# FFN entry of a decoder step: two pairs evicted unscaled, a table loaded earlier, weight sums queued behind an eviction

## The chip, the cores and the metric

The kernel runs on one core of a Trainium2 chip. The metric is the device time of one execution in microseconds. Before the change it is 1154.72 us, the median of three runs (1151.85 to 1155.08).

## The reference, cut to what matters

One layer of a hybrid decoder is computed in float32 for 520 tokens (a prompt of 512 and 8 single samples) of width 1024. A retention branch and a gated spatial branch (whose gate inputs go through Gelu) are merged and added to the residual. The change lies where the feed-forward part begins:

```python
hn = rms_norm(h, norm_ffn_g)                       # h * rsqrt(mean(h*h) + eps) * g, per token
f_gate, f_up = jnp.split(hn @ w_ffn_in, 2, axis=-1) # 1024 -> 2 x 2816
h = h + (silu(f_gate) * f_up) @ w_ffn_down          # 2816 -> 1024
```

Afterwards comes one last RMSNorm.

## The kernel before

**Layout.** Activations lie with features on the 128 partitions and the 520 tokens along the free dimension, in two halves L and R of 260. Every float32 product is three matmuls on split operands (high times high, high times low, low times high). A split is a cast on ScalarE (L87, `whi`, `hxh`) and a subtraction on VectorE (L90, `wlo`, `hxl`).

**Phases near the change.** In order: eight products `ps_gu` with Gelu (L691), `ps_gm`, the merged projection `ps_wo` (its eviction into `hs` is L844), then the feed-forward part. That part has 22 pairs (one block of 128 gate columns and one of 128 up columns each), run as pairs 0 to 9, a down projection `ps_fd`, pairs 10 to 17, a second down phase, pairs 18 to 21, and a third. In a down phase each of eight blocks is evicted by L906 (times the root) and added to `hs` by L907.

**One pair.** `ffn_in(i)` uses a seven-product scheme (Strassen's, on the 2 x 2 blocks of gate and up against the two halves of the model width, with the tokens' halves). `seven` runs seven stages of 12 matmuls each (L822), in the order a, s1, b, s2, s3, s4, d, into three accumulators:

```python
into = dict(a=0, b=2, s1=1, s2=0, s3=0, s4=1, d=0)
```

Banks 0 and 1 are one two-bank tile `ps_f`, of which two exist, bank 2 is a tile of its own, `ps_f3`. Behind each stage `seen` evicts: s1 by L874 (ScalarE), s2 by L876 (ScalarE), b by L872 (VectorE, times the root `rstd`), s3 by L878 (VectorE), s4 by L880 (VectorE), then L881 (GpSimd, times `rstd`, half R) and Silu (L882, ScalarE), d by L884 (ScalarE), and L885 (GpSimd) multiplies gate and up. A stage that writes `ps_f` waits for the eviction of the stage before it, even when that one read the tile's other bank. So s4 waits for L878, and d for L880; stages of the next pair fill such gaps where they are ready.

**Sums of weights.** The scheme needs sums of weight blocks. `sum_weights` loads `ab` and `d` on SP's queue (L747, L749), and `s13` by two SP loads and an adding DMA from GpSimd's queue (L744, L745), and makes `s24` by two additions on VectorE:

```python
nc.vector.tensor_tensor(out=s24[:, 0], in0=s13[:, 0], in1=ab[:, 0], op=ALU.add)      # L753
nc.vector.tensor_tensor(out=s24[:, 1], in0=s24[:, 0], in1=ab[:, 1], op=ALU.add)      # L754
```

`s24`, `s13` and `ab` are split into high and low parts for the stages. There are four buffers of each kind and a pair takes three, in turn. So the cast of a pair's `s24` waits for the buffer of the `s13` of the pair before, which that pair's s3 is the last to read.

**The root.** `row_rstd` (L148 to L155) makes `rstd` from the rows' sums of squares: a scaling on VectorE, Abs_reciprocal_sqrt on ScalarE (L152), and three VectorE instructions that refine it (L153, L154, L155). It is traced behind stage a of pair 0. `rsqrt_table` runs that function on one column so that its table is loaded early. Before, the call that precedes the feed-forward part reads the last Sigmoid's output `sg`; the Gelus, which use another table, run after it.

**Order of work.** Each engine runs its instructions in a fixed order, which a planner writes: it goes through a simulated time, and takes on each engine the earliest traced instruction that is ready. Nothing but data and buffers binds L753, so in the order before, the sums of a pair can stand ahead of evictions of the pair before it. In the order planned, the stages of the entry follow each other as a(0), a(1), s1(0), b(0), b(1) with s2(0), s1(1), s3(0), s4(0), s2(1), d(0), s3(1), a(2). Later pairs alternate between s3(2), s1(3), b(3), s4(2), s2(3), d(2) and s3(3), a(4), s4(3), s1(4), b(4), d(3), s2(4).

Of the kernel before, what the change touches and what calls it, by code (L numbers as in the profile page):

```python
# [7 lines left out]
F32 = mybir.dt.float32  # L8
# [3 lines left out]
ALU = mybir.AluOpType  # L12
# [3 lines left out]
KT = D // P  # L16
NP = 512
NS = 8
T = NP + NS
HT = T // 2  # L20
# [15 lines left out]
def halves(ap):  # L36
    return ap.rearrange("p (a b) -> p a b", a=2)
# [3 lines left out]
def step_kernel(ctx: ExitStack, tc: tile.TileContext, io):  # L41
    nc = tc.nc
# [13 lines left out]
    def ttile(name):  # L56
        return tmp.tile([P, T], F32, name=name, tag="tmp")

    def pair(name):
        return big.tile([P, 2, T], F32R, name=name, tag="big")  # L60
# [7 lines left out]
    def acc_psum(name):  # L68
        return psm.tile([P, 2, 512], F32, name=name, tag="mm")

    def aux(name):
        return psa.tile([P, 512], F32, name=name, tag="aux")
# [4 lines left out]
    def wtile(kind, dt=F32R):  # L77

        pools = wpools[kind]
        pool = pools[wturn[kind] % len(pools)]  # L80
        wturn[kind] += 1
        return pool.tile([P, 8 * P], dt, name=kind, tag=kind, bufs=pools.count(pool))

    def split(hi, lo, src, hi_eng=None, lo_eng=None):

        if hi_eng is None:
            nc.scalar.copy(out=hi, in_=src)  # L87
        else:
            hi_eng.tensor_copy(out=hi, in_=src)
        (lo_eng or nc.vector).tensor_tensor(out=lo, in0=src, in1=hi.bitcast(F32), op=ALU.subtract)  # L90
# [39 lines left out]
    def rsqrt_table(after):  # L130

        one = small.tile([P, 1], F32, name="one", bufs=1)
        nc.scalar.activation(out=one, in_=after[:, 0:1], func=AF.Abs_reciprocal_sqrt)
# [10 lines left out]
    def row_rstd(out, ps, width):  # L144

        y, v, t = (stile(f"rr_{x}") for x in "yvt")
        for f in range(2):
            nc.vector.tensor_scalar(  # L148
                out=v[:, f * HT : (f + 1) * HT], in0=ps[f][:, 0:HT], scalar1=1.0 / width, scalar2=EPS,
                op0=ALU.mult, op1=ALU.add,  # L150
            )
        root = nc.scalar.activation(out=y, in_=v, func=AF.Abs_reciprocal_sqrt)  # L152
        nc.vector.scalar_tensor_tensor(out=t, in0=y, scalar=-0.5, in1=y, op0=ALU.mult, op1=ALU.mult)  # L153
        nc.vector.tensor_tensor(out=t, in0=t, in1=v, op=ALU.mult)  # L154
        nc.vector.scalar_tensor_tensor(out=out, in0=t, scalar=1.5, in1=y, op0=ALU.add, op1=ALU.mult)  # L155
        return root
# [8 lines left out]
    def row_sums(acc):  # L165

        pr = [stile(f"sq{x}", F32R) for x in "hl"]
        split(pr[0], pr[1], acc)
        out = []
        for f in range(2):  # L170
            ps = aux("ps_ss")
            for k in range(2):
                nc.tensor.matmul(
                    ps[:, 0:HT], ones_r, pr[k][:, f * HT : (f + 1) * HT], start=k == 0, stop=k == 1
                )
            out.append(ps)
        return out
# [21 lines left out]
    rstd = const.tile([P, T], F32, name="rstd")  # L199
# [498 lines left out]
    sg = []  # L698
    with tc.tile_pool(name="gp", bufs=1) as gp:
        gm = gmlp(gp)  # L700


    rsqrt_table(sg[-1][:, 1, :])
    mm = []
    for i in range(KT):
        w = weights(io["w_gm_o"][i], KT)
# [3 lines left out]
        s = ttile("ms")  # L710
# [17 lines left out]

    fp = ctx.enter_context(tc.tile_pool(name="fp", bufs=1))

    def sum_weights(src):

        def block(t):
            return t.rearrange("p (a b) -> p a b", a=2)

        def both(t):
            hi, lo = wtile("whi"), wtile("wlo")
            split(hi, lo, t)
            hi, lo = block(hi), block(lo)
            return [(hi[:, i], lo[:, i]) for i in range(2)]  # L740

        s13 = block(wp.tile([P, 8 * P], F32, name="s13", tag="wraw", bufs=3))
        for i in range(2):
            nc.sync.dma_start(out=s13[:, i], in_=src[:, 0])  # L744
        nc.gpsimd.dma_start(out=s13, in_=src[:, 1:3], accum_op=ALU.add)  # L745
        ab = block(wq.tile([P, 8 * P], F32, name="ab", tag="wraw", bufs=2))
        nc.sync.dma_start(out=ab, in_=src[:, 2:4])  # L747
        d = fp.tile([P, 4 * P], F32, name="d", bufs=1)
        nc.sync.dma_start(out=d, in_=src[:, 1])  # L749
        w = dict(zip("a b".split(), both(ab.rearrange("p a b -> p (a b)"))))  # L750
        w |= dict(zip("s1 s3".split(), both(s13.rearrange("p a b -> p (a b)"))))
        s24 = block(fp.tile([P, 8 * P], F32, name="s24", bufs=1))
        nc.vector.tensor_tensor(out=s24[:, 0], in0=s13[:, 0], in1=ab[:, 0], op=ALU.add)  # L753
        nc.vector.tensor_tensor(out=s24[:, 1], in0=s24[:, 0], in1=ab[:, 1], op=ALU.add)  # L754
        w |= dict(zip("s2 s4".split(), both(s24.rearrange("p a b -> p (a b)"))))
        w["d"] = tuple(wq.tile([P, 4 * P], F32R, name=f"wd{x}") for x in "hl")
        split(*w["d"], d)
        return w
# [51 lines left out]
    def seven(w, x, name, seen):  # L810

        ps = acc_psum(name)
        bank = [ps[:, 0, 0:HT], ps[:, 1, 0:HT], aux(f"{name}3")[:, 0:HT]]
        into = dict(a=0, b=2, s1=1, s2=0, s3=0, s4=1, d=0)
        begun = {2}
        for s in ORDER:
            to = into[s]
            acts = x[MEETS[s]]
            for k, (xh, xl) in enumerate(acts):
                sl = slice(k * P, (k + 1) * P)  # L820
                for n, (ww, xx) in enumerate(((w[s][0], xh), (w[s][0], xl), (w[s][1], xh))):
                    nc.tensor.matmul(  # L822
                        bank[to], ww[:, sl], xx, start=to not in begun,
                        stop=k == len(acts) - 1 and n == 2, skip_group_check=True,
                    )
                    begun.add(to)
            if s == "a":
                nc.scalar.copy(out=bank[2], in_=bank[0])
            seen(s, bank)
# [6 lines left out]
    for i in range(KT):  # L836
# [6 lines left out]
        hi = hs[:, i, :]  # L843
# [11 lines left out]
    hx = sum_acts(fill_h, "hx", KT // 2)  # L855
# [2 lines left out]

    rstd = const.tile([P, T], F32, name="rstd")
    act = []  # L860
    L, R = slice(0, HT), slice(HT, T)

    def ffn_in(i):

        a, b = ttile("fa"), ttile("fb")

        def seen(s, bank):
            if s == "a":
                if i == 0:
                    row_rstd(rstd, row_sums(sq), D)  # L870
            elif s == "b":
                nc.vector.tensor_tensor(out=a[:, L], in0=bank[2], in1=rstd[:, L], op=ALU.mult)  # L872
            elif s == "s1":
                nc.scalar.activation(out=b[:, R], in_=bank[1], func=AF.Copy, scale=-1.0)  # L874
            elif s == "s2":
                nc.scalar.copy(out=a[:, R], in_=bank[0])  # L876
            elif s == "s3":
                nc.vector.tensor_tensor(out=b[:, R], in0=b[:, R], in1=bank[0], op=ALU.subtract)  # L878
            elif s == "s4":
                nc.vector.tensor_tensor(out=a[:, R], in0=a[:, R], in1=bank[1], op=ALU.add)  # L880
                nc.gpsimd.tensor_tensor(out=a[:, R], in0=a[:, R], in1=rstd[:, R], op=ALU.mult)  # L881
                nc.scalar.activation(out=a, in_=a, func=AF.Silu)  # L882
            else:
                nc.scalar.activation(out=b[:, L], in_=bank[0], func=AF.Copy, scale=-1.0)  # L884
                nc.gpsimd.tensor_tensor(out=b, in0=a, in1=b, op=ALU.mult)  # L885

        seven(sum_weights(io["w_ffn_in"][i].rearrange("p (s c) -> p s c", s=4)), hx, "ps_f", seen)
        pr = pair(f"act{i}")
        split(pr[:, 0, :], pr[:, 1, :], b)
        act.append(pr)  # L890

    def down(ps, w, k0, n, fs=(0, 1)):
        for k in range(n):
            product(ps, w, k, act[k0 + k], k == 0, k == n - 1, fs)

    def down_weights(i, k0, n):
        return weights(io["w_ffn_down"][i][:, k0 * P : (k0 + n) * P], n)

    def ffn_down(k0, n, last=False):

        for i in range(KT - last):
            ps = acc_psum("ps_fd")
            down(ps, down_weights(i, k0, n), k0, n)
            hi = hs[:, i, :]
            t = ttile("fd")
            nc.vector.tensor_tensor(out=halves(t), in0=ev(ps), in1=halves(rstd), op=ALU.mult)  # L906
            nc.vector.tensor_tensor(out=hi, in0=hi, in1=t, op=ALU.add)  # L907
            if last:

                add_square(sq, hi, i == 0, add=nc.vector)  # L910
                nc.scalar.activation(out=hi, in_=hi, func=AF.Copy, scale=gains[:, 2, i : i + 1])

    done = k0 = 0
    for n in (8, 8, 6):
        for i in range(done, min(k0 + NACT, NF)):
            ffn_in(i)
        done = min(k0 + NACT, NF)
# [8 lines left out]
    i = KT - 1  # L926
    hi = hs[:, i, :]
# [112 lines left out]
```

## Time and profile before

| | |
|---|---|
| median of three runs | 1154.72 us |
| the profiled execution | 1151.46 us |
| its span, first to last instruction | 1149.8 us |
| TensorE busy | 1116.9 us (97%) |
| VectorE busy | 760.9 us (66%) |
| ScalarE busy | 513.5 us (45%) |
| GpSimd busy | 225.1 us (20%) |
| mean granted TensorE clock | 0.989 |

PE is TensorE's matmuls and PEld its weight loads, DVE is VectorE, ACT ScalarE, POOL GpSimd, SP the queue of SyncE. Times count from the first instruction. The feed-forward part begins at about 766 us, its down phases lie at about 873 to 922, 1002 to 1053 and 1097 to 1133 us.

### The profile page before, as it was taken

To read this page: it belongs to the slowest core of one execution; us is meant where nothing else is said; L and a number is where in the kernel's file an instruction comes from. 1 tells how busy PE (TensorE), PEld (TensorE's weight loads), DVE (VectorE), ACT (ScalarE), POOL (GpSimd) and SP (SyncE) were. 2 spreads that over 40 slices of the span, in tenths; PEclk is the share of its full clock that TensorE was granted. 3 is DMA by queue.
4 is the path that set the end of the run, shared out by engine and by line. 5 is a ranking of instruction groups with operands and counts; after the bars stand their busy time and mean duration, and the time that the engine had idled before them with its cause. 6 is when DMAs were issued, how large, how long until landed. Compare 5 with 4: busy or idle time off the path is not lost.

```text
span 1149.8 us, 21702 instructions
## 1 busy us (share of the span) xinstructions
PE 1116.9 (97%) x8982; PEld 1095.4 (95%) x8982; DVE 760.9 (66%) x1223; ACT 513.5 (45%) x837; POOL 225.1 (20%) x198
## 2 busy tenths in 40 slices
PE   8999999999999999999999999998999999999994
PEld 7999999999999999999999999998999999999993
DVE  7777837885788578648534456697786467645754
ACT  6365345533554356323322432465664155522551
POOL 4303201320142011001211222222332013310200
PEclk8999999999999999999999999999999999999998
DMA  7267336733673367222222322665655556445302
GB/s 269 99 233 265 112 111 217 251 111 111 241 245 105 112 231 275 80 94 82 89 79 83 109 80 93 171 137 142 176 150 149 138 126 187 138 122 140 90 18 74
DMA packets 54434, 164.82 MB, mean 143 GB/s; under 512 B 6416, under 2 KB 8864, under 8 KB 54328
## 3 DMA queue, kind: packets, MB, share of 16 engines
q1 hardware_dynamic: 43488, 124.53, 32.7%
q0 software_dynamic: 10848, 38.91, 12.4%
q8 instruction: 70, 1.15, 0.4%
q14 instruction: 28, 0.23, 0.1%
HBM read 142.32 MB, written 21.10 MB: 142 GB/s over the span
## 4 chain that ended last, share of the span: by engine, by line
PE 71%; DVE 12%; DMA 7%; issue 5%; ACT 3%; POOL 1%; SPq 0%; DVEq 0%; ACTq 0%; POOLq 0%
PE ps_f L822 15%; PE ps_fd L108 10%; PE ps_ro L108 8%; PE ps_v L108 7%; PE ps_gu L108 4%; PE ps_ar L108 4%; PE ps_gm L108 4%; PE ps_ag L108 3%; PE ps_gv L108 3%; DVE wlo L90 3%; DMA S<-in_st 3%; PE q L108 2%; PE k L108 2%; PE ps_g L108 2%; PE ps_sc L363 1%
## 5 line engine op out<-in xcount | busy, mean ns | idle before, releaser
L87 ACT CAST whi<-wraw 128x1024 fp32r<-128x1024 f32 (+3 forms) x139 | 141.3, 1018 | 275.2 <-issue 60.1
L90 DVE TENSOR_TENSOR wlo<-wraw,whi 128x1024 fp32r<-128x1024 f32 (+3 forms) x139 | 182.7, 1315 | 33.3 <-ACT whi L87 31.2
L108 PE MATMUL ps_fd<-act,whi 128*128 128x260 f32 x704 | 113.7, 282 | 2.4 <-DVE fd L906 1.8
L822 PE MATMUL ps_f<-hxh,whi 128*128 128x260 f32 x352 | 101.1, 287 | 6.1 <-DVE fb L878 3.9
L108 PEld LDWEIGHTS ps_fd<-act,whi 128*128 128x128 f32 x704 | 96.6, 188 | 3.4 <-ACT whi L87 1.6
L822 PE MATMUL ps_f<-hxh,wlo 128*128 128x260 f32 x352 | 99.3, 284 | 0.6 <-DVE wlo L90 0.6
L822 PE MATMUL ps_f<-hxl,whi 128*128 128x260 f32 x352 | 99.8, 284 | 0.0
L108 PE MATMUL ps_ro<-gated,whi 128*128 128x260 f32 x512 | 82.5, 283 | 0.0
L108 PE MATMUL ps_g<-xg,whi 128*128 128x260 f32 x512 | 82.5, 283 | 0.0
L108 PE MATMUL ps_v<-xg,whi 128*128 128x260 f32 x512 | 82.0, 282 | 0.0
L822 PEld LDWEIGHTS ps_f<-hxh,whi 128*128 128x128 f32 x352 | 66.7, 190 | 8.8 <-DVE fb L878 4.5
L108 PE MATMUL ps_fd<-act,wlo 128*128 128x260 f32 x352 | 71.8, 282 | 0.0
L108 PEld LDWEIGHTS ps_ro<-gated,whi 128*128 128x128 f32 x512 | 70.5, 188 | 0.8 <-issue 0.2
L108 PEld LDWEIGHTS ps_v<-xg,whi 128*128 128x128 f32 x512 | 70.0, 188 | 0.0
L108 PEld LDWEIGHTS ps_g<-xg,whi 128*128 128x128 f32 x512 | 69.8, 188 | 0.0
L822 PEld LDWEIGHTS ps_f<-hxh,wlo 128*128 128x128 f32 x352 | 66.5, 190 | 0.8 <-DVE wlo L90 0.8
L447 ACT ACTIVATE kv<-qkb,vs 128x256 f32<-128x256 f32 x128 | 54.0, 498 | 29.0 <-DMA qkb<-qks 26.0
L822 PEld LDWEIGHTS ps_f<-hxl,whi 128*128 128x128 f32 x352 | 66.7, 190 | 0.0
L90 DVE TENSOR_TENSOR wlo<-s,whi 128x1024 fp32r<-128x1024 f32 x44 | 58.3, 1324 | 12.0 <-ACT whi L87 12.0
L822 PE MATMUL ps_f<-hxm,whi 128*128 128x260 f32 x352 | 65.8, 283 | 0.0
L87 ACT CAST whi<-s 128x1024 fp32r<-128x1024 f32 x44 | 46.1, 1048 | 40.3 <-PE ps_fd L108 20.5
L452 DVE SCALAR_TENSOR_TENSOR junk<-S,qkb 128x256 f32<-128x256 f32 x128 | 53.8, 421 | 2.2
(271 smaller groups left out, 2884.4 us busy)
## 6 DMA issues: line engine op xcount, KB each, us to landing
wraw<-in_w_in SPq DMA_DIRECT2D x78, 512.0 KB, 3.5
S<-in_st SPq DMA_DIRECT2D x32, 512.0 KB, 4.9
out_rss<-S POOLq DMA_DIRECT2D x32, 512.0 KB, 3.9
s<-in_w_ffn_in SPq DMA_DIRECT2D x44, 256.0 KB, 4.2
s<-in_w_ffn_in POOLq DMA_DIRECT2D x22, 512.0 KB, 6.3
ab<-in_w_ffn_in SPq DMA_DIRECT2D x22, 512.0 KB, 4.4
qkb<-qks POOLq DMA_DIRECT2D x16, 512.0 KB, 5.0
wraw<-in_w_ret_o SPq DMA_DIRECT2D x16, 512.0 KB, 3.5
```

The source lines that it names most:

```text
L87: nc.scalar.copy(out=hi, in_=src)
L90: (lo_eng or nc.vector).tensor_tensor(out=lo, in0=src, in1=hi.bitcast(F32), op=ALU.subtract)
L108: nc.tensor.matmul((ps[f] if isinstance(ps, list) else ps[:, f])[:, 0:HT], a, x[:, k, f * HT : (f + 1) * HT], start=first and n == 0, stop ...
L363: nc.tensor.matmul(ps[:, 0:n], a[:, d, s * P : (s + 1) * P], b[:, d, s * P : NP], start=i == 0, stop=i == 5)
L447: nc.scalar.activation(out=kv[:, j, :], in_=kb, func=AF.Copy, scale=vs[:, j, b : b + 1])
L452: nc.vector.scalar_tensor_tensor(out=junk, in0=S[:, j, :], scalar=1.0, in1=qb, op0=ALU.mult, op1=ALU.mult, accum_out=os_[:, j, b : b + 1],)
L822: nc.tensor.matmul(bank[to], ww[:, sl], xx, start=to not in begun, stop=k == len(acts) - 1 and n == 2, skip_group_check=True,)
```

## The change

- The early table load now reads the low half of the last Gelu's product, so it comes behind the last Gelu.
- For pairs 0 and 1, L872 copies bank 2 without `rstd`; L881 then multiplies all 520 columns of `fa` by `rstd`, and not the R half alone.
- L878's instructions are kept in a list, with the L907 of the second last block of each down phase (the last one before the special end in the third). The first addition of a pair's `s24` (L753) is ordered, on VectorE's queue alone, behind the last entry of that list when the pair is traced. For pairs 1 to 9, 11 to 17 and 19 to 21 that is the L878 of the pair before; for pairs 10 and 18 it is that L907. Pair 0 has none.

```diff
-    rsqrt_table(sg[-1][:, 1, :])
+    rsqrt_table(gm[-1][:, 1, :].bitcast(F32))
...
-    def sum_weights(src):
+    def sum_weights(src, behind):
...
-        nc.vector.tensor_tensor(out=s24[:, 0], in0=s13[:, 0], in1=ab[:, 0], op=ALU.add)
+
+        with tc.issue_after(behind.ins) if behind else nullcontext():
+            nc.vector.tensor_tensor(out=s24[:, 0], in0=s13[:, 0], in1=ab[:, 0], op=ALU.add)
...
+    evicted = []
...
             elif s == "b":
-                nc.vector.tensor_tensor(out=a[:, L], in0=bank[2], in1=rstd[:, L], op=ALU.mult)
+                if i < 2:
+                    nc.vector.tensor_copy(out=a[:, L], in_=bank[2])
+                else:
+                    nc.vector.tensor_tensor(out=a[:, L], in0=bank[2], in1=rstd[:, L], op=ALU.mult)
...
             elif s == "s3":
-                nc.vector.tensor_tensor(out=b[:, R], in0=b[:, R], in1=bank[0], op=ALU.subtract)
+                evicted.append(nc.vector.tensor_tensor(out=b[:, R], in0=b[:, R], in1=bank[0], op=ALU.subtract))
             elif s == "s4":
                 nc.vector.tensor_tensor(out=a[:, R], in0=a[:, R], in1=bank[1], op=ALU.add)
-                nc.gpsimd.tensor_tensor(out=a[:, R], in0=a[:, R], in1=rstd[:, R], op=ALU.mult)
+                cols = slice(0 if i < 2 else HT, T)
+                nc.gpsimd.tensor_tensor(out=a[:, cols], in0=a[:, cols], in1=rstd[:, cols], op=ALU.mult)
                 nc.scalar.activation(out=a, in_=a, func=AF.Silu)
...
-        seven(sum_weights(io["w_ffn_in"][i].rearrange("p (s c) -> p s c", s=4)), hx, "ps_f", seen)
+        seven(sum_weights(io["w_ffn_in"][i].rearrange("p (s c) -> p s c", s=4), evicted and evicted[-1]), hx, "ps_f", seen)
...
-            nc.vector.tensor_tensor(out=hi, in0=hi, in1=t, op=ALU.add)
+            done = nc.vector.tensor_tensor(out=hi, in0=hi, in1=t, op=ALU.add)
+            if i == KT - 2:
+                evicted.append(done)
```

## Rows read from the trace of the kernel before

**Rows 1.** The page, busy time, share of the span and instructions by engine.

```profile
PE 1116.9 (97%) x8982; PEld 1095.4 (95%) x8982; DVE 760.9 (66%) x1223; ACT 513.5 (45%) x837; POOL 225.1 (20%) x198
```

**Rows 2.** Busy time by stretch: length, PE, PEld, DVE, ACT, POOL; clock, DMA share, GB/s.

```profile
766.00:776.00 10.00, 8.30 (x68) 7.91 (x67) 8.55 (x17) 6.88 (x15) 0.99 (x1) 1.00 0.50 105
776.00:780.80 4.80, 4.80 (x42) 4.70 (x40) 2.20 (x4) 2.94 (x4) 0.00 (x0) 1.00 0.38 109
780.80:783.70 2.90, 0.12 (x1) 0.00 (x0) 2.87 (x6) 1.53 (x3) 0.85 (x1) 1.00 0.25 23
783.70:787.20 3.50, 3.44 (x16) 3.44 (x17) 2.85 (x7) 0.64 (x1) 0.00 (x0) 0.52 0.70 136
792.00:873.00 81.00, 80.82 (x670) 80.19 (x670) 61.26 (x77) 48.79 (x79) 27.09 (x21) 1.00 0.60 160
```

**Rows 3.** Timeline of TensorE: start, duration, instruction, [idle before, releaser].

```profile
769.32 0.36 PE L822 MATMUL ps_f<-hxh,whi 128*128 128x260 f32 x1 [1.14 <-DVE hs L844]
...
770.36 0.39 PE L822 MATMUL ps_f<-hxh,wlo 128*128 128x260 f32 x1 [0.56 <-DVE wlo L90]
...
783.76 0.59 PE L822 MATMUL ps_f<-hxh,whi 128*128 128x260 f32 x1 [2.85 <-DVE fb L878]
...
934.84 0.39 PE L822 MATMUL ps_f<-hxh,whi 128*128 128x260 f32 x1 [0.52 <-DVE fb L878]
...
1035.77 0.72 PE L108 MATMUL ps_fd<-act,whi 128*128 128x260 f32 x4 [1.46 <-DVE fd L906]
```

**Rows 4.** Timeline of VectorE ahead of the entry.

```profile
764.46 0.69 DVE L753 TENSOR_TENSOR s<-s,ab 128x512 f32<-128x512 f32 x1
...
767.55 0.68 DVE L754 TENSOR_TENSOR s<-s,ab 128x512 f32<-128x512 f32 x1
...
768.49 0.68 DVE L844 TENSOR_TENSOR hs<-ps_wo,xr 128x520 f32<-128x520 f32 x1
```

**Rows 5.** Timeline of ScalarE: the kernel's start, behind the last Gelu, the entry.

```profile
4.24 0.64 ACT L161 ACTIVATE sq<-xt 128x520 f32<-128x520 f32 x1 [0.76 <-DMA xt<-in_xT]
...
680.84 1.05 ACT L87 CAST whi<-wraw 128x1024 fp32r<-128x1024 f32 x1 [3.26 <-PE ps_gm L108]
...
777.83 0.38 ACT L876 COPY fa<-ps_f 128x260 f32<-128x260 f32 x1 [2.17 <-PE ps_f L822]
778.23 1.28 ACT L152 ACT_TABLE_LOAD   x1
```

**Rows 6.** Timeline of VectorE at the entry, from the root on.

```profile
780.20 0.70 DVE L153 SCALAR_TENSOR_TENSOR rr_t<-rr_y 128x520 f32<-128x520 f32 x1 [2.60 <-ACT rr_y L152]
...
781.55 1.22 DVE L90 TENSOR_TENSOR wlo<-ab,whi 128x1024 fp32r<-128x1024 f32 x1
782.68 0.69 DVE L155 SCALAR_TENSOR_TENSOR rstd<-rr_t,rr_y 128x520 f32<-128x520 f32 x1
783.29 0.42 DVE L878 TENSOR_TENSOR fb<-fb,ps_f 128x260 f32<-128x260 f32 x1
...
784.76 0.75 DVE L872 TENSOR_TENSOR fa<-ps_f,rstd 128x260 f32<-128x260 f32 x2
```

**Rows 7.** GpSimd's products (min/median/max ns), its addition at the entry, VectorE beside it.

```profile
L881 POOL TENSOR_TENSOR fa<-fa,rstd x22: 744/1128/1666, 787.3 to 1096.9; 128x260 f32<-128x260 f32 x22
L885 POOL TENSOR_TENSOR fb<-fa,fb x22: 1302/1472/1786, 791.7 to 1099.1; 128x520 f32<-128x520 f32 x22
765.38 1.61 POOL L163 TENSOR_TENSOR sq<-sq,sqr 128x520 f32<-128x520 f32 x1
765.07 2.22 DVE L788 TENSOR_TENSOR xsum<-xsum 128x260 f32<-128x260 f32 x1
```

**Rows 8.** Timelines of ScalarE and VectorE behind s3 of pair 2: split of pair 3's s24.

```profile
803.28 1.05 ACT L87 CAST whi<-s 128x1024 fp32r<-128x1024 f32 x1 [0.70 <-PE ps_f L822]
804.37 1.23 DVE L90 TENSOR_TENSOR wlo<-s,whi 128x1024 fp32r<-128x1024 f32 x1 [0.54 <-ACT whi L87]
```

**Rows 9.** Timeline of VectorE in the second down phase.

```profile
1033.59 0.69 DVE L753 TENSOR_TENSOR s<-s,ab 128x512 f32<-128x512 f32 x1 [8.18 <-DMA s<-in_w_ffn_in]
```

## The prediction

> **What bounds the kernel now.** The page comes first: TensorE is busy 1116.9 of 1149.8 us [rows 1], so only the roughly 33 us in which it isn't, and stretches in which it runs slowly, can be won without taking matmuls away. VectorE's 66% is no second bound over the whole span. The reader then goes to the busy times by stretch: between 792 and 873 us, with pairs 2 to 9 in flight, TensorE is busy 80.82 of 81 us with 670 matmuls, 0.1206 us each [rows 2]. A stage of 12 matmuls is therefore 1.45 us, and a steady pair has nothing to give. The entry is different: 8.30 busy of 10 us (766 to 776), 0.12 of 2.90 (780.8 to 783.7), and then 16 matmuls in 3.44 us at a granted clock of 0.52, which is the 1.2 GHz level [rows 2].
>
> TensorE's own timeline names the waits: 1.14 us for hs (L844) and 0.56 us for a wlo, both ahead of stage a of pair 1; 2.85 us for fb (L878), the eviction of s3 of pair 0, ahead of its s4; later 0.52 us for the same eviction at the first pair of a group, and 1.46 us for an fd inside the second down phase [rows 3]. These are the places the change touches. The rest, at the kernel's start and end, it leaves alone.
>
> **The change part by part.** All sums go against the profiled execution (1151.46 us, span 1149.8); the median of the three timed runs is 1154.72, 3.26 above it. I apply the difference to the median.
>
> *Sums off VectorE before the entry.* L753 and L754 of pair 1 stand at 764.46 and 767.55, ahead of the L844 at 768.49 for which TensorE waits [rows 4]. Pair 1's sums are now ordered behind L878 of pair 0, so 0.69 + 0.68 = 1.37 us leave that queue. At most 1.37 of the 1.14 + 0.56 = 1.70 us of waiting goes; at least nothing, if waits for ScalarE's scaled parts fill the hole. I take 1.0, nearer the full queue time, as VectorE is busy 8.55 of these 10 us [rows 2]. Everything after it in the entry moves up with it.
>
> *Table.* On ScalarE the load for the root takes 1.28 us at 778.23, between L876 and the root [rows 5]; VectorE idles 2.60 us for the root [rows 6]. With the table loaded behind the last Gelu this 1.28 us goes. The load itself moves to about 678 us, where ScalarE idles 3.26 us before the cast at 680.84 [rows 5]; that hides it at no cost, and without that gap it would delay one cast by 1.28 us, once. The load behind the last Sigmoid disappears, with none on TensorE's path. That no other load comes between needs Square, the casts and Copy to run under the root's table; at the kernel's start the Square at 4.24 does so without one [rows 5].
>
> *L878 of pair 0.* Its place: L153 at 780.20, a wlo of pair 2 at 781.55, L155 at 782.68, L878 at 783.29 [rows 6]. The pause of 2.85 us shrinks by 1.28 to 1.57 if the order stays. If the wlo (1.13 us to the next start) is put elsewhere, it shrinks to about the bare eviction, 0.52 [rows 3]. Between 1.57 and 0.52 I take 1.0: a gain of 1.85 us (1.28 to 2.33).
>
> *Clock.* After the 2.85 us pause the granted clock is 0.52 and 16 matmuls take 3.44 us [rows 2]. At 0.1206 they take 1.93, so 1.5 us were lost. Ahead of 776 us two pauses of 1.14 and 0.56 left the clock at 1.00 [rows 2, 3], so with a pause of 1.0 the whole 1.5 should come back (bounds 0 and 1.5).
>
> *Copies in place of products.* The two L872 (0.75 us together at 784.76) stand behind L878, with no wait of TensorE behind them [rows 6]. As copies of the same 260 columns out of PSUM they need no root and may run in VectorE's idle 2.60 us. I cost this at nothing; if one lands in front of L878 it costs 0.42.
>
> *The wider product on GpSimd.* For pairs 0 and 1 L881 goes from 260 to 520 columns. The nearest rows are L881 (0.74 at least, median 1.13) and the 520-wide L885 (1.30 at least, median 1.47) [rows 7]. Some 0.35 to 0.56 us more each lies ahead of Silu and, behind that on ScalarE, of the last eviction of the pair. I cost it at zero since stage s2 of pair 1 now runs in that time, and keep 0.56 in the range.
>
> *The wait added at the entry.* This is what the change pays. Behind L878 (0.42) now queue L753 and L754 (0.69 + 0.68) [rows 4, 6], then the cast of their high half (1.05) and the low half (1.23) [rows 5, 8]: the lo weights of s2 of pair 1 are ready 4.07 us after s3 of pair 0 ends. Now TensorE does s4, s2 of pair 1, d; then s2 isn't ready after s4, and d has to come first, behind its own eviction: 0.52 + 1.45 + 0.52 + 1.45 = 3.94 us, and s2 waits 0.13 more. The price is 0.52 + 0.13 = 0.65 us; at best 0.5, and 1.7 where a wlo of 1.23 cuts into the chain on VectorE. Entry together: -1.0 - 1.85 - 1.5 + 0.65 = -3.7.
>
> The Trainium skill speaks against the cheap view of the wider product: its page "SBUF — State Buffer", sections "SBUF: two separate sides" and "Who interferes with whom", has GpSimd and a VectorE instruction with two SBUF operands take turns on one port pair, the later fully blocked. The trace agrees in kind: L788 takes 2.22 us over 260 columns, against 0.42 for L878, while GpSimd's L163 runs from 765.38 for 1.61 [rows 6, 7]; but by the records VectorE had begun first. By this rule a sum or wlo of pair 1 would stand still for the whole wider product, and the total below would shrink from 3.4 to 1.9; that is the rival on the port.
>
> *Down phases.* In the second, VectorE waits 8.18 us on L753 of pair 18 for a load, with fd behind it [rows 9], and TensorE loses 1.46 [rows 3]. Pair 18's sum now stands behind the second last L907 of the phase, when the load has long landed: -1.46 (at worst 0, if another wait takes its place). At the starts of groups two and three (pairs 10 and 18), pairs 11 and 19 repeat the entry's added wait: 2 x 0.65 = +1.3 (0 to 2.6).
>
> *Steady pairs.* Already before, the cast of a pair's s2/s4 weights waits for s3 of the pair before (803.28, as its buffer frees), and the low half ends at 805.60 [rows 8]: 2.32 us. Now 0.42 + 0.69 + 0.68 stand in front: 4.11 us. In the order of now, odd pairs have three stages in between (4.35 us), even ones five; d of the pair before can stand in as a fourth (5.80). It fits, by 0.24 to 1.69 us, with other casts in the queues. Pairs 2 to 9, 12 to 17, 20 and 21 are 16: between 0 and 16 x 0.52 = 8.3 us. I take 0.5 in sum, near the lower end, since the order is planned with these waits known. Loads that wait until the sums free their buffers (ab, s13) go out later too, on SP's queue and GpSimd's; no steady pair waits long for anything [rows 2], so I cost that at nothing, and a load that comes late belongs to the starved rival.
>
> Sum: -3.7 - 1.46 + 1.3 + 0.5 = -3.4 us: 1151.3 us on the median's scale, 1148.1 for the profiled execution.
>
> **The rivals.** *The entry opens wholly* and no start of a group pays: -1.37 - 2.33 - 1.5 + 0.5 - 1.46 = -6.2, 1148.5 us. For it speaks VectorE's idle time around the root; against it that 4.07 us of weights stand against 3.94 of other work.
>
> *The sums starve s2.* Each of the 16 steady pairs waits once for a bare eviction or for its weights, 0.52 each: -3.7 - 1.46 + 1.3 + 8.3 = +4.4, 1159.1 us. It turns the result from 3.86 / 16 = 0.24 us a pair on, and 0.24 us is just the slack of odd pairs. Against it: d can be drawn forward, and VectorE is busy only 61.26 of 81 us [rows 2].
>
> *The pause is only cut into pieces:* L878 stays behind the wlo (1.28 gained), d and s2 wait at the 1.7 end, and with 3 us of pauses close together the clock falls anyway: -1.0 - 1.28 + 1.7 - 1.46 + 1.3 + 0.5 = -0.2, 1154.5 us. Against it: 1.70 us in two pieces did not lower the clock. This is the case in which the change doesn't do what it says.
>
> *The port:* a sum or wlo of pair 1 waits out the 520-wide product, 1.30 to 1.79 us [rows 7], say 1.5: -1.9, 1152.8 us. Against it: the product starts after s4's eviction, when the sums should be through.
>
> **How the numbers follow.** Forecast 0.40, wholly open 0.25, starved 0.13, pieces 0.12, port 0.10. About what a measurement tells from no change is 0.3%, 3.46 us, and the forecast lies on that line, so half of it counts as faster: 0.20 + 0.24 + 0.02 = 0.46 faster. Slower is 0.11 of the starved case and 0.02 of the others, 0.13. The rest, 0.41, is the same. The forecast's own range is 1149.5 to 1153.2; the range, with the open case and most of the others, is 1147.5 to 1156.
>
> **What would show it.** Right: no table load before L152 and one near 678 us; a pause of 0.5 to 1.6 us before s4 of pair 0; clock 1.00 from 783 to 787; d of pair 0 ahead of s2 of pair 1 with waits near 0.5; no wait for fd near 1035; 80 us or more busy of the 81 in the steady stretch. Wrong: L878 still 2.5 us late, a second clock drop, or TensorE waiting for wlo or whi in most pairs.

## The result and the profile after

The changed kernel takes 1159.12 us (median of 7 runs, 1157.89 to 1165.02) beside 1151.85 for the kernel before (7 runs): ratio 1.0079, interval 1.0056 to 1.0102. It is slower by 0.8%. The forecast of 1151.3 stood on the median of three runs, 1154.72; it is a ratio of 0.9970, or 1148.4 us on the median of seven. Run again later, beside other kernels, the changed kernel gave 1.0084 (e10).

TensorE's busy time and the busy times by stretch, as in [rows 1, 2]:

```profile
PE 1123.0 (97%) x8982; PEld 1097.2 (95%) x8982; DVE 757.6 (65%) x1223; ACT 510.1 (44%) x836; POOL 222.9 (19%) x198
```

```profile
766.00:776.00 10.00, 9.45 (x79) 9.24 (x78) 9.42 (x18) 7.59 (x18) 2.18 (x2) 1.00 0.36 62
776.00:788.00 12.00, 9.83 (x80) 9.41 (x79) 9.02 (x16) 4.96 (x7) 0.88 (x1) 1.00 0.08 18
792.00:873.00 81.00, 78.83 (x632) 76.12 (x631) 57.95 (x76) 45.20 (x74) 24.14 (x22) 1.00 0.64 160
```

The entry's clock now stays at 1.00. But between 792 and 873 us, where TensorE did 670 matmuls before [rows 2], it does 632: the steady pairs have become slow. At 0.1206 us a matmul the missing 38 are 4.6 us.

ScalarE at the last Gelu and at the root, VectorE from the root on, GpSimd's first product of the entry and VectorE beside it, as in [rows 5 to 7]:

```profile
681.23 1.28 ACT L133 ACT_TABLE_LOAD   x1
...
684.47 1.05 ACT L87 CAST whi<-wraw 128x1024 fp32r<-128x1024 f32 x1 [1.74 <-issue]
...
780.15 0.38 ACT L882 COPY fa<-ps_f 128x260 f32<-128x260 f32 x1 [2.17 <-PE ps_f L824]
780.42 0.64 ACT L152 ACTIVATE rr_y<-rr_v 128x520 f32<-128x520 f32 x1
...
781.71 0.42 DVE L876 COPY fa<-ps_f 128x260 f32<-128x260 f32 x1
...
784.40 0.42 DVE L884 TENSOR_TENSOR fb<-fb,ps_f 128x260 f32<-128x260 f32 x1
...
787.12 1.32 POOL L888 TENSOR_TENSOR fa<-fa,rstd 128x520 f32<-128x520 f32 x1 [17.45 <-DVE fa L886]
...
787.32 3.34 DVE L90 TENSOR_TENSOR wlo<-s,whi 128x1024 fp32r<-128x1024 f32 x2 [0.27 <-ACT whi L87]
```

The table load lies in idle time, and the root follows its neighbour without one.

TensorE's waits from the entry on, as in [rows 3]:

```profile
772.67 0.39 PE L824 MATMUL ps_f<-hxh,wlo 128*128 128x260 f32 x1 [0.55 <-DVE wlo L90]
...
784.88 0.39 PE L824 MATMUL ps_f<-hxh,whi 128*128 128x260 f32 x1 [1.65 <-DVE fb L884]
...
787.10 0.51 PE L824 MATMUL ps_f<-hxm,wdh 128*128 128x260 f32 x2 [0.52 <-DVE fa L886]
...
789.58 0.39 PE L824 MATMUL ps_f<-hxm,wlo 128*128 128x260 f32 x1 [0.53 <-DVE wlo L90]
...
804.82 0.39 PE L824 MATMUL ps_f<-hxh,whi 128*128 128x260 f32 x1 [0.82 <-ACT fb L891]
...
826.12 0.39 PE L824 MATMUL ps_f<-hxh,whi 128*128 128x260 f32 x1 [0.39 <-ACT fb L891]
...
847.50 0.39 PE L824 MATMUL ps_f<-hxh,whi 128*128 128x260 f32 x1 [0.47 <-ACT fb L891]
...
942.18 0.51 PE L824 MATMUL ps_f<-hxm,wdh 128*128 128x260 f32 x2 [0.52 <-DVE fa L886]
...
949.42 0.39 PE L824 MATMUL ps_f<-hxh,whi 128*128 128x260 f32 x1 [0.90 <-ACT ps_f L830]
```

The wait for hs is gone, the pause ahead of s4 is 1.65 us and not 2.85, and the 1.46 for fd does not come again. New are d and s2 at 787 and 789, and three waits for L891, the last eviction of a pair, ahead of a3, a5 and a7 (stage a of pairs 3, 5 and 7).

The line numbers are those of the changed kernel: L755/L756 the sums, L876 the copy and L878 the product in place of L872, L880 to L886 the evictions of s1 to s4, L888 GpSimd's first product, L889 Silu, L891 the eviction of d, L892 GpSimd's second product.

**A ledger.** From the first matmul of the feed-forward part to the last of the profile, in us, measured between starts of matmuls ("again" is e10; entry: until s4 of pair 1 and s1 and b of pair 2 are through; steady: until s2 of pair 9 and d of pair 8 are; the stretch from there to a of pair 10 is 50.5 in before and 50.2 after):

| stretch | before | after | again | forecast, change | measured, change |
|---|---|---|---|---|---|
| entry | 30.75 | 28.58 | 28.03 | -3.7 | -2.2, -2.7 |
| steady, group one | 74.32 | 78.20 | 78.75 | +0.2 | +3.9, +4.4 |
| pair 10 to 18 | 130.92 | 133.47 | 134.26 | -0.6 | +2.5, +3.3 |
| pair 18 to the end | 86.80 | 90.09 | 90.02 | +0.7 | +3.3, +3.2 |
| all | 373.33 | 380.58 | 381.30 | -3.4 | +7.3, +8.0 |

(The forecast's 0.5 for steady pairs is split 8 : 6 : 2 over the groups.) The profiled execution, 1162.47, also lost some 4 us at about 450 us, where the program is unchanged; the last section tells of that.

**The new waits.** In the steady stretch of group one, TensorE's pauses above 0.05 us (start of a matmul less the start before it, less 0.1195) are these:

| kernel | ahead of s2 | of d | of a | sum |
|---|---|---|---|---|
| before | 0 | 0 | 0.99 | 0.99 |
| after | 1.05 | 1.08 | 2.80 | 4.93 |
| after, again | 1.05 | 1.07 | 3.37 | 5.49 |

How they come about shows in pairs 1 and 2, engine by engine: VectorE, SP's queue, GpSimd, ScalarE.

```profile
794.92 0.42 DVE L884 TENSOR_TENSOR fb<-fb,ps_f 128x260 f32<-128x260 f32 x1
795.25 0.69 DVE L755 TENSOR_TENSOR s<-s,ab 128x512 f32<-128x512 f32 x1
...
798.11 2.35 DVE L90 TENSOR_TENSOR wlo<-s,whi 128x1024 fp32r<-128x1024 f32 x2
800.38 0.42 DVE L886 TENSOR_TENSOR fa<-fa,ps_f 128x260 f32<-128x260 f32 x1
...
795.96 0.80 SPq L744 DMA_DIRECT2D s<-in_w_ffn_in  x2
...
801.10 0.87 POOL L745 DMA_DIRECT2D s<-in_w_ffn_in  x1 [7.49 <-DVE fa L886]
801.68 1.62 POOL L888 TENSOR_TENSOR fa<-fa,rstd 128x520 f32<-128x520 f32 x1
...
803.34 0.64 ACT L889 ACTIVATE fa<-fa 128x520 f32<-128x520 f32 x1 [2.08 <-POOL fa L888]
803.88 0.60 ACT L87 CAST wdh<-d 128x512 fp32r<-128x512 f32 x1
804.39 0.38 ACT L891 ACTIVATE fb<-ps_f 128x260 f32<-128x260 f32 x1
```

The same chain in the kernel before:

```profile
789.52 0.80 SPq L744 DMA_DIRECT2D s<-in_w_ffn_in  x2
...
794.70 0.86 POOL L745 DMA_DIRECT2D s<-in_w_ffn_in  x1 [1.53 <-DVE wlo L90]
795.88 1.13 POOL L881 TENSOR_TENSOR fa<-fa,rstd 128x260 f32<-128x260 f32 x1 [0.32 <-DVE fa L880]
```

L745 (here pair 5's) adds onto what the two loads L744 bring, and starts 5.14 us after them here, 5.18 before. L744 needs the buffer that the sum L755 frees, so the later sum holds L745 back: at 801.10, where the product L888 of pair 1 has stood behind it since its operand was ready at 800.80 (800.38 + 0.42). The profile names L886 as what L745 waited for; that instruction touches no data of the load, and in the second profile the same wait, 7.92 us, is put down to the DMA. Then come Silu, a cast and L891, and a3 starts after 0.82 us of idle time. The low halves (798.11) in turn hold L886 up, and so d.

### The profile page after: what moved, and what is told of

The parts are those of the page before. It is cut to its first block, busy times and chain, and to the rows that moved or that the text cites. A ratio compares the mean times of both kernels' runs of the same rounds, so it can differ in the third digit from the quotient of the medians.

```text
span 1160.8 us, 21686 instructions
## 1 busy us (share of the span) xinstructions
PE 1123.0 (97%) x8982; PEld 1097.2 (95%) x8982; DVE 757.6 (65%) x1223; ACT 510.1 (44%) x836; POOL 222.9 (19%) x198
## 4 chain that ended last, share of the span: by engine, by line
PE 83%; DVE 5%; DMA 4%; ACT 3%; issue 2%; POOL 2%; SPq 0%; DVEq 0%; ACTq 0%; POOLq 0%
PE ps_f L824 15%; PE ps_fd L108 11%; PE ps_ro L108 8%; PE ps_v L108 8%; PE ps_g L108 6%; PE ps_gu L108 4%; PE q L108 4%; PE k L108 4%; PE ps_ar L108 4%; PE ps_gm L108 4%; PE ps_ag L108 3%; PE ps_gv L108 3%; PE ps_o L465 2%; PE ps_s L481 1%; PE ps_sc L363 1%
```

## The experiments

Three theories stood at first: WAIT (each steady pair pays for sums behind the eviction), ORDER (the wait at the first pair makes the planner shift the order of stages by a pair, and that costs), PRODUCT (the wider product on GpSimd costs). All ratios are to the kernel before on the same chip, with their 95% interval. SILU and GPSIMD, in the expectations of later runs, name the place of Silu on ScalarE's queue and that of the adding load on GpSimd's.

**e1, the table and the copies without ordered sums.** `evicted and evicted[-1]` becomes `None`.

> Edits one and two alone (table behind the last Gelu; unscaled evictions of pairs 0 and 1 with the wider product); no sum is ordered behind an eviction. Theory WAIT (each pair's s2 waits for sums that come late): the steady pairs run as before, the entry gains 3 to 5 us, total -3 to -5 us against before. Theory ORDER (one late sum at the second pair of a group makes the planner interleave the pairs in another, worse pattern): the planned order of stages is that of before, so the same -3 to -5 us. Theory PRODUCT (the 520-wide product on GpSimd blocks VectorE and delays Silu): the loss stays, 0 to +4 us.

Measured 1148.60, 0.9968 (0.9945 to 0.9992). The steady stretch is as before, with 0.96 us of waits ahead of a. PRODUCT falls: edits one and two bring a gain, the third turns it into a loss.

**e2, the ordered sums alone.** The table and L872's product are put back as before, and `cols = R`.

> Edit three alone: sums ordered behind evictions, evictions and table as before. In the planned order pairs 3 to 9 interleave as before the change, pairs 11 on as in the changed kernel. WAIT: from pair 0's first stage to pair 10's first stage it loses as the changed kernel does in its steady pairs, 3 to 4 us against the 155.6 of before, and again 2.6 and 3.3 in the other groups; total +7 to +11 us. ORDER: the first group loses under 1.5 us, the second and third groups lose as in the changed kernel (133.5 against 130.9, 89.5 against 86.2 us); total +4 to +7 us. PRODUCT: no loss, -1.5 to 0 us.

Measured 1166.10, 1.0121 (1.0098 to 1.0145). TensorE's timeline, then its busy time by stretch:

```profile
785.49 0.39 PE L824 MATMUL ps_f<-hxh,whi 128*128 128x260 f32 x1 [2.85 <-DVE fb L881]
...
787.95 0.80 PE L824 MATMUL ps_f<-hxm,wdh 128*128 128x260 f32 x2 [0.52 <-DVE fa L883]
```

```profile
785.00:800.00 15.00, 13.30 (x74) 12.70 (x74) 6.73 (x11) 6.50 (x11) 2.92 (x3) 0.66 0.50 123
```

Without the other edits the 2.85 us pause is back, with a wait behind it that was not there before, and the clock is 0.66 over 15 us. The entry takes 34.50 us for 30.75, which no theory had counted, and so the whole loss, 13.2 us, lies above the 7 to 11 of WAIT. The steady waits are 5.67 us, though this kernel's stages stand in the order of before in group one: WAIT holds without ORDER.

**e3, ordered sums for pairs 10 and 18 alone** (`evicted[-1] if i in (10, 18) else None`).

> Edits one and two, and sums ordered behind an eviction for pairs 10 and 18 alone (behind the second last addition of the down phase). All of the pairs' planned order is that of before. WAIT and ORDER: entry -3 to -5 us, and the 1.46 us wait for an fd in the second down phase goes: -4.5 to -6.5 us in all, second group 129.4 us. PRODUCT: +1 or more in the first group.

Measured 1145.81, 0.9944 (0.9925 to 0.9963): faster than both kernels. Steady waits 0.98 us; the 1.46 us for fd are gone.

**e4, ordered sums for pair 1 alone** (`evicted[-1] if i == 1 else None`).

> Edits one and two, and the sum ordered behind an eviction for pair 1 alone; the sums of all other pairs are free. The planner interleaves pairs 1 to 9 as in the changed kernel, and pairs 10 on as before. WAIT: only pair 1 pays, so the first group (pair 0's first stage to pair 10's) takes 152 to 154 us and the total is -2 to -4 us. ORDER: the first group takes about 157 us as in the changed kernel, groups two and three as before (130.9 and 86.2), total +1 to +2 us.

Measured 1155.31, 1.0021 (1.0002 to 1.0041). The steady waits are 7.12 us (a 3.34, d 3.78), with all sums after pair 1 free but the stages in the shifted order. So ORDER seemed to hold as well. GpSimd, ScalarE, VectorE and TensorE show what it was:

```profile
803.58 0.86 POOL L745 DMA_DIRECT2D s<-in_w_ffn_in  x1 [5.19 <-DMA s<-in_w_ffn_in]
804.17 1.60 POOL L892 TENSOR_TENSOR fb<-fa,fb 128x520 f32<-128x520 f32 x1
...
805.80 0.62 ACT L87 CAST act<-fb 128x520 fp32r<-128x520 f32 x1 [3.79 <-POOL fb L892]
...
806.46 0.70 DVE L90 TENSOR_TENSOR act<-fb,act 128x520 fp32r<-128x520 f32 x1 [3.68 <-ACT act L87]
807.08 0.42 DVE L886 TENSOR_TENSOR fa<-fa,ps_f 128x260 f32<-128x260 f32 x1
...
807.55 0.51 PE L824 MATMUL ps_f<-hxm,wdh 128*128 128x260 f32 x2 [1.62 <-DVE fa L886]
```

The adding load waits 5.19 us on GpSimd's queue, and four instructions on three engines queue up behind it.

**e5, Silu behind the last eviction of its pair, in the changed kernel.**

```diff
-                nc.scalar.activation(out=a, in_=a, func=AF.Silu)
             else:
-                nc.scalar.activation(out=b[:, L], ...)
+                gone = nc.scalar.activation(out=b[:, L], ...)
+                with tc.issue_after(gone.ins):
+                    nc.scalar.activation(out=a, in_=a, func=AF.Silu)
```

> The changed kernel, with ScalarE's Silu of each pair put behind the last eviction of that pair (d), which in the changed kernel stands behind it; the stages on TensorE keep the changed kernel's order through the steady stretch. Theory WAIT, in its second form: of the 4.93 us that TensorE waits in the steady stretch of group one, the 2.80 in front of the a stages are the d eviction, held on ScalarE by a Silu that waits for GpSimd's product, which waits for the weights' sums to be through; these 2.80 us and their like in groups two and three go, some 5 to 6 us, and the 2.1 us in front of s2 and d stay: ratio to the kernel before about 1.003, some 1154 to 1155 us. Theory ORDER: the a stages come too late through the order of the stages itself, whatever stands on ScalarE: 1158 to 1160, ratio 1.006 or more.

Measured 1154.18, 1.0009 (0.9993 to 1.0025), below the 1.003 of WAIT. The waits ahead of a are gone (0 for 2.80); s2 keeps 1.26, and d falls from 1.08 to 0.26, for a reason that no run shows. Pair 10 to 18 takes 130.90 us and pair 18 to the end 89.01. So with every sum where the change puts it, moving one instruction of each pair on ScalarE takes nearly the whole loss back (1.0009 for 1.0079 and 1.0084). GpSimd, then ScalarE:

```profile
794.61 0.87 POOL L745 DMA_DIRECT2D s<-in_w_ffn_in  x1 [7.74 <-DVE fa L886]
...
796.25 0.38 ACT L890 ACTIVATE fb<-ps_f 128x260 f32<-128x260 f32 x1
796.86 0.64 ACT L892 ACTIVATE fa<-fa 128x520 f32<-128x520 f32 x1 [0.23 <-POOL fa L888]
```

The load waits as long as before (7.74), and the product stands behind it, but the eviction, here L890, no longer queues behind Silu (L892).

**e6, free sums for pairs 1, 11 and 19, ordered ones elsewhere** (`None if i in (0, 1, 11, 19)`).

> The changed kernel, with the sums of pairs 1, 11 and 19 left free, as in the kernel before, and those of all other pairs behind the eviction (pairs 10 and 18 behind the down phase's add). The entry and the order of the stages of group one are then those of the kernel without any ordered sum. Theory WAIT: each of the 16 steady pairs pays, whatever the order of the stages: 4.7 us in group one, as in the run with the ordered sums alone, and 16 x 0.59 = 9.4 in all, from the 1145.8 of the run with pairs 10 and 18 alone to some 1155, ratio about 1.003. Theory ORDER: only the shift of the order that the wait at the first pairs brings costs; without it the steady pairs are free, as in the sum on record: 1146 to 1148, ratio 0.994 to 0.996.

Measured 1152.08, 1.0003 (0.9980 to 1.0027), between the two numbers expected. Group one has 3.98 us of waits in the order of before (s2 1.05, d 1.07, a 1.86), as WAIT has it; groups two and three take 130.69 and 87.03 us, hardly more than with free sums (130.01 and 86.74 in e3). Not each of the 16 pairs pays.

**e7, the table alone, and e8, the copies and the wider product alone**, in the kernel before.

> The kernel before with the table's load alone moved behind the last Gelu. By the steps on record: 1.28 us less in front of s4 of pair 0, a pause of 1.57, and with it the clock's 1.5 us: -2.8, ratio 0.9976. Rival: the shorter pause still drops the clock, -1.3, ratio 0.9989.

> The kernel before with the copies for the first two pairs and GpSimd's wider product alone; the table loads where it did, between an eviction of the entry and the root. By the steps on record the copies cost and bring nothing, and the clock falls as before: 0, ratio 1.000. Rival: with the products gone the work is put in another order, part of s2 of pair 1 ahead of s4 of pair 0, as in the run without ordered sums, which covers the pause whatever the table does: -2 to -4 us, ratio 0.997 to 0.998.

Measured 1148.64, 0.9967 (0.9948 to 0.9986), and 1150.40, 0.9986 (0.9969 to 1.0003). TensorE's wait ahead of s4 and the stretch 776 to 788 us, e7 and then e8:

```profile
782.37 0.39 PE L822 MATMUL ps_f<-hxh,whi 128*128 128x260 f32 x1 [1.43 <-DVE fb L878]
```

```profile
776.00:788.00 12.00, 10.57 (x89) 10.36 (x88) 10.13 (x15) 6.68 (x10) 1.98 (x2) 1.00 0.52 113
```

```profile
780.09 0.51 PE L824 MATMUL ps_f<-hxm,whi 128*128 128x260 f32 x2 [1.45 <-ACT whi L87]
...
781.70 0.59 PE L824 MATMUL ps_f<-hxh,whi 128*128 128x260 f32 x1 [1.09 <-DVE fb L884]
```

```profile
776.00:788.00 12.00, 9.45 (x64) 9.03 (x63) 8.83 (x11) 6.91 (x9) 2.54 (x2) 0.86 0.53 109
```

The table's move alone shortens the entry by 3.04 us (30.75 to 27.71) and keeps the clock. The copies alone only cut the 2.85 us in two (1.45 and 1.09 with part of s2 between), the clock falls, and the entry is 30.57.

**e9, e3 with the late Silu.**

> The run with ordered sums for pairs 10 and 18 alone, with ScalarE's Silu put behind the last eviction of its pair as well. Theory SILU: the waits in front of stage a that are left there in the steady stretches (0.98 us in group one, 1.56 in group two) have the same origin as the changed kernel's, the last eviction behind a waiting Silu; they go, 2.5 us: ratio to the kernel before about 0.992, some 1143 us. Rival: they come from weights, and nothing moves: 0.994 to 0.995.

Measured 1145.71, 0.9945 (0.9923 to 0.9967): the waits ahead of a go, as theory SILU had it, but the time is its rival's. The ledger from pair 0 on is 365.40 us for e3's 369.02. The time does not tell this from e3: the two intervals overlap, and in this profile what lies before pair 0 took 3.7 us longer.

**e10, the changed kernel again.**

> The changed kernel once more, unaltered, beside the two others of this set, so that prices are read on one chip, with a second profile. If the late weights near 450 us in its first profile (3.40 us of waiting) were chance, they are not here again and the execution is shorter by 3 to 5 us; the waits of the steady stretch of group one (4.93 us, of them 2.80 in front of a) come again. If they come with the change, both come again. Ratio as before, 1.006 to 1.010.

Measured 1159.87, 1.0084 (1.0059 to 1.0108). The waits came again; the wait at about 450 us was 1.01 us and not 3.40. The profiled execution was no shorter all the same (span 1162.3), as the clock fell at 545 us instead.

**e11, e4 with the late Silu.**

> The run with the ordered sums for pair 1 alone (free sums after that, but the stages in the shifted order), with ScalarE's Silu behind the last eviction of its pair. Theory SILU: of the 7.12 us of waits in the steady stretch of group one, the 3.34 in front of a have the same origin and go, and the 3.78 in front of d, an eviction held on VectorE, stay: ratio about 0.999, some 1151 us. Theory ORDER: the shifted order costs whatever stands on ScalarE: 1.002 again.

Measured 1152.02, 1.0007 (0.9991 to 1.0023). The waits ahead of a went (3.34 to 0), but those ahead of d grew from 3.78 to 5.52 (2.65 and 2.87). Behind the second the granted clock was 0.57 from 831 to 835 us, which adds some 1.5: 7.05 in all. Silu's place only moved the price; its origin lay further up.

**e12 to e14, the adding load behind a product on GpSimd's queue.** `made` collects GpSimd's products, L888 in e12 and L892 in e13 and e14:

```diff
-        nc.gpsimd.dma_start(out=s13, in_=src[:, 1:3], accum_op=ALU.add)
+        with tc.issue_after(made[-4].ins) if len(made) > 3 else nullcontext():
+            nc.gpsimd.dma_start(out=s13, in_=src[:, 1:3], accum_op=ALU.add)
```

e12 is the changed kernel with it:

> The changed kernel, with GpSimd's adding load of s13 for pair i (L745) put behind GpSimd's product of pair i-4 (L888) on its queue; in the changed kernel the loads of pairs 5, 7 and 9 stand in front of the products of pairs 1, 3 and 5. Theory GPSIMD: L745 adds onto what SP's two loads of the same pair (L744) bring, these go out only when the sums free the buffer, and the product, Silu and the d eviction queue behind that wait; the waits in front of a3, a5, a7 (2.80 and 3.37 us in group one in the two profiles, 1.91 and 2.76 in group two) go, some 5 us, and the 2.1 us in front of s2 and d stay: ratio 1.002 to 1.004. Rival: only Silu's place on ScalarE counts: the a waits stay, 1.007 to 1.009.

Measured 1157.99, 1.0050 (1.0031 to 1.0069), between the two again. GpSimd, and VectorE beside it:

```profile
797.39 2.22 POOL L891 TENSOR_TENSOR fa<-fa,rstd 128x520 f32<-128x520 f32 x1 [7.28 <-DVE fa L889]
799.56 0.86 POOL L748 DMA_DIRECT2D s<-in_w_ffn_in  x1
...
797.23 1.22 DVE L90 TENSOR_TENSOR wlo<-ab,whi 128x1024 fp32r<-128x1024 f32 x1
```

The product now starts when its operand is there, but takes 2.22 us. The waits ahead of a fall to 1.83 us: TensorE still idles 0.61 ahead of a3 (0.82 and 1.25 in the two profiles of the changed kernel), and 0.05 ahead of a5, a7 and a9, as little as in the kernel before; s2 and d keep 2.15. So of the 1.81 and 2.38 us by which the waits ahead of a had grown (2.80 and 3.37 less 0.99) the load's wait was 0.97 and 1.54. The rest stands at a3, behind the wide product of pair 1. Both parts reach TensorE through Silu's place in front of the eviction: in e5 both are gone.

e13 is e4 with it:

> The run with ordered sums for pair 1 alone, with the adding load of pair i behind GpSimd's second product of pair i-4 (L892). The stages keep the shifted order. Theory GPSIMD: the 7.1 us of waits in the steady stretch of group one, d's as much as a's, come from that load's wait on GpSimd's queue; under 2 us are left: ratio 0.996 to 0.998. Theory ORDER: the shifted order itself costs, as it did with Silu moved: 6 to 7 us of waits again, ratio 1.001 to 1.002.

Measured 1147.94, 0.9967 (0.9952 to 0.9983). GpSimd's queue at the place shown for e4:

```profile
801.91 1.54 POOL L895 TENSOR_TENSOR fb<-fa,fb 128x520 f32<-128x520 f32 x1 [1.54 <-ACT fb L894]
803.40 0.85 POOL L748 DMA_DIRECT2D s<-in_w_ffn_in  x1
```

Of 7.12 us of waits 1.85 are left, none ahead of d, in the same order of stages. ORDER falls: what cost in e4 was the place of a load on GpSimd's queue.

e14 is e3 with it:

> The run with ordered sums for pairs 10 and 18 alone, with the adding load of pair i behind GpSimd's second product of pair i-4 (L892). Theory GPSIMD: the 0.98 and 1.56 us in front of a that are left in groups one and two have this origin too and go: 0.992 to 0.993. Rival: they come from Silu's place alone, or the later load now comes too late for its own pair: 0.994 to 0.996.

Measured 1146.50, 0.9960 (0.9938 to 0.9982). In group one the 0.98 us stay, as the rival had it; in group two 1.56 become 0.66. The time does not tell it from e3's: the intervals overlap.

## Why the prediction was wrong, step by step

*Sums off VectorE before the entry, -1.0.* Held: 1.70 us of waits became 0.55 (0.49 in the second profile; up to 1.02 in e12, which orders the sums alike).

*Table, -1.28 (a part of the next term), and clock, -1.5.* Held: the table's move alone measured 3.04 us of the entry, and the clock stays at 1.00 with 2.70 us of pauses in three pieces between 783 and 790.

*L878 of pair 0, 1.85 taken of 1.28 to 2.33.* Too much: the wlo stayed in front (782.65, L884 at 784.40), 2.85 became 1.65, a gain of 1.20 and so less than the 1.28 of the lower bound. With the table alone the pause is 1.43 (e7); the other 0.22 is the copy L876, which runs at 781.71 between the root's instructions, ahead of L884.

*Copies and wider product, 0.* Not quite: 0.22 for that copy (0.42 was named for the case), and the wide product has a part in the next term and in the 0.61 us ahead of a3 in e12. By themselves they can't be told from nothing: e8's interval holds 1.000, and its entry is 0.18 us shorter.

*The wait added at the entry, 0.65.* It was 0.52 + 0.53 = 1.05, and in the first profile alone 0.41 more ahead of s1 of pair 2. s2 came 0.53 late and not 0.13, as the two low halves took 3.34 us while the wide product ran (2.35 at 798.11). That is the rival on the port, with 1.0 us in place of 1.5. The Trainium skill's page "SBUF — State Buffer", section "SBUF: two separate sides", says that of a VectorE instruction with two inputs in SBUF and a GpSimd instruction whichever starts first keeps the shared ports and the other waits. Here GpSimd began first (787.12) and VectorE paid; in e12 VectorE began first (797.23) and GpSimd's product took 2.22 us. Both agree with it; L788 of [rows 7], which by the records began first and still took 2.22, does not.

*Down phases, -1.46.* Held for the second: the wait for fd is gone. What it is worth is less clear. e3, which has this besides e1's edits, takes 130.01 us from pair 10 to 18 for e1's 130.85, a gain of 0.84, as other waits there grew; its median is 2.8 us lower, but the intervals of the two ratios overlap. In the third phase the changed kernel's waits ahead of fd grew by 0.7 (1.51 to 2.24).

*Group starts, +1.3.* Low, within its bounds: d of pairs 10 and 18 waits 0.52 each, s1 of pair 12 0.90, 1.94 in all. The d of the last pair waits 0.52 more (1107.84), which no term had.

*Steady pairs, +0.5. This is the step that failed,* and with it the sentence that loads "go out later too, on SP's queue and GpSimd's; no steady pair waits long for anything, so I cost that at nothing". I counted the chain from the eviction through the sums to s2's low weights, 4.11 us, against the stages between, and that chain is late by only 0.13 us a pair (1.05 / 8). I did not follow the other chain that starts at the sums: L744's loads, 5.14 us, the adding load on GpSimd, and the pair's product, Silu and last eviction queued behind it, up to stage a two pairs on. The forecast gave group one a half of the 0.5; its waits grew by 3.9 and 4.5 us. Of that the a stages have 1.8 and 2.4 (2.80 and 3.37 less 0.99), at the end of this chain: e12 and e13 show the load's part in it and e5 Silu's. d has 1.1, as the low halves of the later sums hold L886 up, and s2 1.05. That the planner knew the waits was no ground for a low price: it put L745 of pairs 5, 7 and 9 in front of the products of pairs 1, 3 and 5, in before and after alike, where a later load costs.

*The rival "The sums starve s2"* named 1159.1, and that the measured median is 1159.12 is luck: the rival forecast +4.4 us on 1154.72, and the change measured +7.3 on 1151.85 (+9.1 by ratio). Nor is it the mechanism: s2 pays a quarter of the 0.52 a pair that it charged, and groups two and three pay little in e6, where the starts of the groups are free.

What stays open: why the ordered sums cost so little in groups two and three in e6 (in group two s2 and d wait 1.59 us there, but a only 0.82 for e3's 1.57), and how much of a's price without any ordered sum (0.98 us in group one) is Silu's place alone; e9 takes it to zero, but its time does not show it.

## What to carry to other kernels

Before an instruction is moved behind another, list everything its end releases, and follow each release through the queues to the stage that the bound engine waits for. A load that is freed later can stand on an engine's queue in front of arithmetic that has nothing to do with it. Look too at what stands in front of the instruction that the bound engine waits for: here one Silu handed the delay on. Of three edits in one change only the first paid by the times (the third took 0.84 us out of one stretch in e3): separate them before judging the whole.

## What the runs showed that was not expected

**The same pause lowers the clock in one execution and not in another.** TensorE's pause of 1.23 to 1.24 us ahead of ps_mix, at about 545 us, is in every profile. The stretch 540 to 552 us in the kernel before, and in the changed kernel's second profile:

```profile
540.00:552.00 12.00, 10.77 (x92) 10.63 (x91) 11.64 (x19) 4.28 (x5) 7.13 (x3) 1.00 0.26 89
```

```profile
540.00:552.00 12.00, 10.77 (x69) 10.63 (x69) 11.50 (x19) 4.28 (x5) 7.10 (x3) 0.75 0.27 89
```

The granted clock is 1.00 and 0.75, and 23 matmuls fewer fit into 12 us; in e3 and e7 it is 0.86. In the changed kernel's first profile it was another place: weights came late, the cast `sqh` stood behind theirs on ScalarE, and TensorE waited for it. That wait is 0.31 us in the kernel before, and 2.52 in e9, where the clock stayed at 1.00 from 446 to 460 us; here it is 3.40, and the mean clock over these 14 us is 0.76.

```profile
453.81 0.80 PE L173 MATMUL ps_ss<-sqh,ones_r 128*128 128x260 f32 x2 [3.40 <-ACT sqh L87]
```

```profile
446.00:460.00 14.00, 10.60 (x67) 10.39 (x67) 9.15 (x12) 5.30 (x7) 4.24 (x4) 0.76 0.62 222
```

So one profile's total differs from another's by 3 to 4 us in places that no edit touched (the feed-forward part begins at 762.76 us in e6 and at 766.25 in e3), as much as the whole effect looked for. The ledger of the stretch that was changed agrees with the timed ratios better: within 2.2 us in all 15 profiles (after +7.3 and +8.0 by ledger, +9.1 and +9.7 by ratio; e7 -3.7 and -3.8; at worst e1, -1.5 and -3.7), where the profiled times are off by up to 4.6 (e6).
